# One scratch tile per FFN block and four smaller placements in a hybrid encoder layer

## The chip, the cores and the metric

The kernel runs on one NeuronCore of a Trainium2 chip. The metric is the device time of one execution in microseconds, as the median of the runs. The engines are named as in the profile: PE is TensorE's matmul stream and PEld its weight loads, DVE is VectorE, ACT is ScalarE, POOL is GpSimd, SP is SyncE, which here only issues transfers. Each engine works through its own instructions in order and waits on semaphores for the others. Transfers that SP issues run on the DMA queue q1, those that POOL issues on q0, and those that ACT issues on q10. All share the core's 16 DMA engines.

## The reference, cut to what matters

Two request groups (256 and 512 tokens, 768 rows in all, D = 1024) go through one encoder layer with the same weights:

```
h = RMSNorm(x);  u, q, k, v, qm, gl = split(h @ w_in)
z = gelu(bidirectional S5 scan of u + d*u)
s5_out   = z * sigmoid(z @ s5_w_glu)
diff_out = differential attention(q, k, v)          # 8 heads
mem_out  = cross-attention(qm, memory)              # 4 heads
merged   = sum over the branches n of sigmoid(gl[n] + b) * (out[n] @ w_branch[n])
x  = x + merged @ w_out                             # residual rows
h2 = RMSNorm(x);  g, up = split(h2 @ w_gate_up)     # 2 x 2816 columns
x  = x + (silu(g) * up) @ w_down                    # 2816 x 1024
```

## The kernel before

Everything is float32. A product is done as three matmuls on operands that are split into a high and a low part (`mm3`, lines 751 to 753: high by high, high by low, low by high). `split_evac` (lines 742 to 746) makes such a pair: ACT writes the high part, DVE the low part as the difference. In this way z becomes zhi and zlo, a left factor of the down projection dxh and dxl, its weights whd and wld. Activations are kept by features: a tile has 128 partitions and 8 blocks of 768 tokens.

The Tile framework places tiles in pools and puts the instructions of each engine in an order by its own simulation of the time. A pool that opens over SBUF bytes of an older pool inherits that pool's last users: the first tile of the new pool waits for all of them.

**The middle of the kernel.** Branch 2 (the memory branch, `br` over H) runs while differential attention is finished beside it. `finish(h)` transposes a head's output on PE (`oT`, line 1333), scales it on ACT into the tile `do` (line 1334), and ACT issues its store to the scratch `br_scr` (line 1335). Then comes the GLU of the S5 branch, `glu = z @ s5_w_glu`: `load_pair` loads the eight z tiles from scratch (names `brr`, POOL's queue, line 1525), half through the pool zst and half through the pool stg, and splits them. One `brr` buffer is free again when DVE has made its zlo. The `zs` tiles are z once more for the product with the sigmoid. After that come branch 0 (`br` over the GLU's result, with `glr` tiles of gates on POOL's queue), branch 1 (over xd, the differential attention's output loaded back from `br_scr`), the output projection `wo` and the FFN. The residual rows x1 (six tiles of 512 KB, line 1563) are needed at `wo`.

**The FFN and the down projection.** Eleven blocks of the hidden layer are made one after the other. POOL does the last products of a block in its tile `fa` (pool ffa, two buffers), and SP stores it to the scratch `hid_scr` (`hid_store`, line 1425). The down projection is a Strassen-like scheme: the 768 tokens are two halves r, the 22 feature groups of 128 two halves kh, the output columns two halves, and seven products P1, P5, P6, P3, P7, P2, P4 take the place of eight. Each product has six granules g of up to two feature groups. For a granule `a_load` loads a piece of the hidden layer (`da{r}{kh}_{g}`, from `hid_scr`, SP's queue), `w_fetch` loads a piece of w_down and may add a second piece to it with an accumulating load on POOL's queue (line 1733): the tiles `dch` for P5, P6 and P4, `dwr` for the others. `make` forms and splits the factors, AHEAD granules before PE needs them, and the matmuls `dn` take the left factor as the stationary operand and 512 weight columns as the moving one. FETCH says how many granules ahead weights are loaded. Granules 0 to 2 of P1 have their own small pool (dae) and are loaded while the last FFN block runs; all other da tiles lie in the pool downa, which opens when the FFN's pools close.

```
GRAN = [(k, min(2, NFB - k)) for k in range(0, NFB, 2)]
nc.sync.dma_start(t, hid_scr[:, NFB * kh + k0 : NFB * kh + k0 + n, HT * r : HT * r + HT])
load_pair(Z, z_scr, 0.5, (2, 3, 4, 7))
```

Of the kernel before, what the change touches and what calls it, by code (L numbers as in the profile page):

```python
# [8 lines left out]
F32 = mybir.dt.float32  # L9
# [477 lines left out]
TOK = 768  # L487
SEGS = ((0, 256), (256, 512))
TILES = 6
# [137 lines left out]
def hybrid_block(ctx, tc, A, outs, consts):  # L627
    nc = tc.nc
    v, act, gp, pe = nc.vector, nc.scalar, nc.gpsimd, nc.tensor
# [4 lines left out]
    xs = [A["x_prompt"][0, 128 * i : 128 * i + 128] for i in range(2)]  # L634
# [81 lines left out]
    NFB = DFF // 256  # L716
    wd = A["w_down"].rearrange("(k p) c -> p k c", p=128)
# [106 lines left out]
    k2 = qctx.enter_context(tc.tile_pool(name="ma2", bufs=2, side="right"))  # L824
# [3 lines left out]
    y_scr = [dr.tile([128, 8 * 97], F32, name=f"y_scr{m}") for m in range(8)]  # L828
    z_scr = [dr.tile([128, TOK], F32, name=f"z_scr{m}") for m in range(8)]
    gl_scr = [dr.tile([128, TOK], F32, name=f"gl_scr{m}") for m in range(24)]  # L830
    hid_scr = dr.tile([128, 2 * NFB, TOK], F32, name="hid_scr")
    br_scr = [dr.tile([128, TOK], F32, name=f"br_scr{m}") for m in range(8)]
    mo_scr = [dr.tile([128, 8, TOK], F32, name=f"mo_scr{w}") for w in "hl"]

# [136 lines left out]
    with tc.tile_pool(name="nrm", bufs=1) as pool, tc.tile_pool(name="nrmg", bufs=1) as pg:  # L971
# [274 lines left out]
    def diff_attend():  # L1246
# [79 lines left out]

        def finish(h):
            osb = X.pop(("h", h))[0]
            do = stg.tile([128, TOK], F32, name=uid("do"), tag="do", bufs=1)
            for t0, t1 in ((0, 2), (2, 6)):  # L1330
                ps = env.psb("oT")
                for t in range(t0, t1):
                    pe.transpose(ps[:, 128 * (t - t0) : 128 * (t - t0) + 128], osb[:, t], env.ident)
                act.activation(do[:, 128 * t0 : 128 * t1], ps[:, 0 : 128 * (t1 - t0)], AF.Copy, scale=subg)
            act.dma_start(br_scr[h], do)
# [75 lines left out]
    HT = TOK // 2  # L1411
# [10 lines left out]
        eng.tensor_tensor(out=o, in0=o, in1=c, op=mul)  # L1422

    def hid_store(fb):
        nc.sync.dma_start(hid_scr[:, 2 * fb : 2 * fb + 2, :], act_in.pop(fb))

    def new_block(what, fb):
        if what == "gate":
# [51 lines left out]
    with ExitStack() as c5:  # L1480
# [35 lines left out]
                                               in1=MG[0][:, M].bitcast(F32), op0=mul, op1=sub)  # L1516

        zctx = c5.enter_context(ExitStack())
        zst = zctx.enter_context(tc.tile_pool(name="zst", bufs=2, side="right"))

        def load_pair(X, src, scale=None, more=()):
            for m in range(8):
# [36 lines left out]
                split_evac(S[0][:, M], S[1][:, M], t, 0.25)  # L1559
        Xd = pair(XB, "xd")  # L1560
        load_pair(Xd, br_scr)
        for t in range(TILES):
            gp.dma_start(x1[t], xs[t])
        branch(0, S)
        MG = pair(XA, "mgd")
        branch(1, Xd, MG=MG)
        mgctx.close()
# [121 lines left out]


    P1, P5, P6, P3, P7, P2, P4 = range(7)
    GRAN = [(k, min(2, NFB - k)) for k in range(0, NFB, 2)]
    NG = len(GRAN)
    ITEMS = [(p, g) for p in range(7) for g in range(NG)]
    AHEAD, FETCH = 2, 4
    EARLY = 3
    de = ctx.enter_context(ExitStack())
    da_f = de.enter_context(tc.tile_pool(name="daf", bufs=3, side="right"))
    da_e = de.enter_context(tc.tile_pool(name="dae", bufs=1, side="right"))
    DP, a_raw, ch, w_raw, parts = {}, {}, {}, {}, {}  # L1700

    def a_load(q, g):

        k0, n = GRAN[g]
        r, kh = q
        early = q == (0, 0) and g < EARLY
        t = (da_e if early else DP["a"]).tile([128, 2, HT], F32, name=f"da{r}{kh}_{g}")[:, 0:n]
        nc.sync.dma_start(t, hid_scr[:, NFB * kh + k0 : NFB * kh + k0 + n, HT * r : HT * r + HT])
        a_raw[q, g] = t

    def w_quarter(kh, f, g):
        k0, n = GRAN[g]
        return wd[:, NFB * kh + k0 : NFB * kh + k0 + n, 512 * f : 512 * f + 512]

    def w_fetch(i):

        if i >= len(ITEMS):
            return
        p, g = ITEMS[i]
        n = GRAN[g][1]  # L1720
        view = lambda t: t.rearrange("p (k c) -> p k c", k=2)[:, 0:n]
        if p in (P5, P6, P4):
            if p == P5:
                ch[g] = view(DP["ch"].tile([128, 1024], F32, name=f"dch{g}"))
                nc.sync.dma_start(ch[g], w_quarter(0, 0, g))
            t = ch[g]
            src, acc = None, {P5: (0, 1), P6: (1, 1), P4: (1, 0)}[p]
        else:
            t = view(W.praw.tile([128, W.HALF], F32, name=f"dwr{i}", tag="wr"))
            src, acc = {P1: ((0, 0), None), P3: ((1, 1), None), P7: ((0, 1), (1, 1)), P2: ((1, 0), None)}[p]  # L1730
            nc.sync.dma_start(t, w_quarter(*src, g))
        if acc:
            gp.dma_start(t, w_quarter(*acc, g), accum_op=add)
        w_raw[i] = t

    def make(i):
# [1 line left out]
        if i >= len(ITEMS):  # L1738
            return
        p, g = ITEMS[i]  # L1740
        n = GRAN[g][1]
        t = w_raw.pop(i)
        wh, wl = (x.rearrange("p (k c) -> p k c", k=2)[:, 0:n] for x in W.tiles(f"d{i}"))
        split_evac(wh, wl, t)
# [23 lines left out]
        parts[i] = xh, xl, wh, wl  # L1768

    def down_early():  # L1770
        for i in range(FETCH - 1):
            w_fetch(i)
        for g in range(EARLY):
            a_load((0, 0), g)
        for i in range(AHEAD):
            make(i)
# [6 lines left out]
    xbctx.close()  # L1783

    with ExitStack() as c7:
        for k, n in (("a", 1), ("ch", 1), ("t", 2)):
            DP[k] = c7.enter_context(tc.tile_pool(name="down" + k, bufs=n))
        loads = [((0, 0), g) for g in range(EARLY, NG)]
        loads += [(q, g) for g in range(NG) for q in ((1, 0), (1, 1))] + [((0, 1), g) for g in range(NG)]
# [2 lines left out]
        acc = {}  # L1792
        for _ in range(NG - EARLY):
            a_load(*loads.pop(0))
        w_fetch(FETCH - 1)
        for i, (p, g) in enumerate(ITEMS):
            for _ in range(3):
                if loads:
# [4 lines left out]
            if g == 0 and p in (P1, P5, P2):  # L1803
                acc[bank] = [PS[bank].tile([128, 512], F32, name=uid("dn"), tag=bank) for _ in range(3)]
            ps = acc[bank]
            n = GRAN[g][1]
            xh, xl, wh, wl = parts.pop(i)
            for t in range(3):
                c = slice(128 * t, 128 * t + 128)
# [55 lines left out]
```

## Time and profile before

| | |
|---|---|
| time, median of 3 runs | 1800.16 us (1799.32 to 1803.69) |
| the profiled execution | 1803.27 us, of which the span of the trace is 1801.5 us |
| PE busy | 1751.7 us, 97% of the span |
| DVE, ACT, POOL busy | 1263.3, 886.6, 281.4 us |
| moved by DMA | 236.98 MB, 132 GB/s on average |
| q1 (SP), q0 (POOL) | 166.93 MB and 65.02 MB |

In the timeline a row has its start in us from the start of the span, its length, the engine and source line, and the operation as output <- input; in brackets the idle time before it and what ended that. A matmul's length runs to its modelled end, so the pace is read from one start to the next. The chain of waits follows back what released each instruction. A window's row gives for each engine the busy time and the count of instructions, then the granted clock of PE as a share of full speed, the share of the DMA engines and the GB/s.

### The profile page before, as it was taken

Reading aid. Unit: us, or ns where it says so; the run is one execution under the profiler, and the core shown is the slowest. Engines: PE = TensorE matmul, PEld = TensorE weight load, DVE = VectorE, ACT = ScalarE, POOL = GpSimd, SP = SyncE. Lnnn points to the kernel's source line nnn. Section 1 sums busy time; section 2 is a strip of 40 time slices with the busy share of each in tenths; the row PEclk is TensorE's granted clock in tenths of the full one; section 3 lists DMA queues with packets and bytes.
Section 4 is the critical chain, followed back from the end, with each engine's and each line's share of the span. In section 5 each row is a group of like instructions: output and inputs, shape, how many; then the busy total and the mean of one; then the engine's idle time right before and its main releaser. Section 6 shows DMA issues by size and latency. Waiting matters only on the chain.

```text
span 1801.5 us, 29429 instructions
## 1 busy us (share of the span) xinstructions
PE 1751.7 (97%) x11194; PEld 1611.7 (89%) x11194; DVE 1263.3 (70%) x2342; ACT 886.6 (49%) x1856; POOL 281.4 (16%) x300
## 2 busy tenths in 40 slices
PE   9999999999999999999989899999999999996999
PEld 9999988999999999999979788888889999994877
DVE  6665659699999688888865435452797777764854
ACT  6444444677676267777755333232343333332442
POOL 0000000000000001011100101000136555541210
PEclk9999999999999999999999899999999999997999
DMA  7223745664565565454843535322223232349781
GB/s 264 71 83 106 141 110 138 150 160 119 146 154 139 139 168 146 93 112 107 192 127 100 193 105 181 115 94 70 71 85 123 88 117 90 107 164 300 144 204 47
DMA packets 211166, 236.98 MB, mean 132 GB/s; under 512 B 57929, under 2 KB 173393, under 8 KB 211025
## 3 DMA queue, kind: packets, MB, share of 16 engines
q1 hardware_dynamic: 185584, 166.93, 30.5%
q0 software_dynamic: 24288, 65.02, 16.9%
q10 hardware_dynamic: 1152, 3.15, 0.5%
q8 instruction: 88, 1.44, 0.3%
q14 instruction: 54, 0.43, 0.1%
HBM read 168.66 MB, written 41.22 MB: 117 GB/s over the span
## 4 chain that ended last, share of the span: by engine, by line
PE 52%; DMA 5%; DVE 4%; issue 2%; ACT 1%; POOL 0%; SPq 0%; DVEq 0%; ACTq 0%; POOLq 0%
PE br L752 4%; PE br L751 4%; PE br L753 3%; PE up L751 3%; PE up L752 3%; PE up L753 3%; PE gate L751 3%; PE gate L753 3%; PE gate L752 3%; PE dn L751 2%; PE dn L753 2%; PE dn L752 2%; PE av L1311 2%; PE qk L752 2%; PE qk L751 2%
## 5 line engine op out<-in xcount | busy, mean ns | idle before, releaser
L595 ACT ACTIVATE wh<-wr 128x1024 fp32r<-128x1024 f32 x124 | 140.4, 1133 | 63.3 <-PE br L752 18.1
L601 DVE TENSOR_TENSOR wl<-wr,wh 128x1024 fp32r<-128x1024 f32 x82 | 108.3, 1324 | 81.3 <-ACT wh L595 79.4
L751 PE MATMUL gl<-Hhi,wh 128*128 128x256 f32 (+1 forms) x384 | 133.0, 346 | 2.3 <-ACT glt L1114 2.3
L753 PE MATMUL gl<-Hhi,wl 128*128 128x256 f32 (+1 forms) x384 | 129.7, 338 | 0.0
L752 PE MATMUL gl<-Hlo,wh 128*128 128x256 f32 (+1 forms) x384 | 129.4, 337 | 0.0
L751 PE MATMUL qk<-wh,Hhi 128*128 128x256 f32 x384 | 108.7, 283 | 0.7 <-ACT V L1210 0.7
L752 PE MATMUL qk<-wl,Hhi 128*128 128x256 f32 x384 | 109.3, 285 | 0.0
L751 PE MATMUL dn<-whd,dxh 128*128 128x512 f32 x231 | 92.5, 402 | 17.3 <-ACT dxh L745 17.3
L753 PE MATMUL qk<-wh,Hlo 128*128 128x256 f32 x384 | 108.5, 283 | 0.0
L599 POOL DMA_DIRECT2D wl<-wr x42 | 36.6, 872 | 454.8 <-ACT wl L598 427.7
L752 PE MATMUL dn<-wld,dxh 128*128 128x512 f32 x231 | 92.4, 401 | 0.1
L753 PE MATMUL dn<-whd,dxl 128*128 128x512 f32 x231 | 89.8, 400 | 0.7 <-DVE dxl L746 0.7
L751 PEld LDWEIGHTS gl<-Hhi,wh 128*128 128x128 f32 x384 | 72.8, 190 | 9.7 <-ACT glt L1114 2.7
L753 PEld LDWEIGHTS gl<-Hhi,wl 128*128 128x128 f32 x384 | 72.7, 189 | 8.0
L752 PEld LDWEIGHTS gl<-Hlo,wh 128*128 128x128 f32 x384 | 72.9, 190 | 7.2
L1280 DVE TENSOR_REDUCE nm<-sc 128x1 f32<-128x512 f32 (+1 forms) x96 | 56.5, 598 | 26.2 <-PE sc L1275 25.1
L751 PEld LDWEIGHTS qk<-wh,Hhi 128*128 128x128 f32 x384 | 73.2, 191 | 1.6 <-ACT V L1210 0.9
L753 PEld LDWEIGHTS qk<-wh,Hlo 128*128 128x128 f32 x384 | 73.4, 191 | 0.3
L752 PEld LDWEIGHTS qk<-wl,Hhi 128*128 128x128 f32 x384 | 72.9, 190 | 0.6
L557 ACT ACTIVATE wh_S<-ws 128x512 fp32r<-128x512 f32 x70 | 41.1, 625 | 59.5 <-PE up L752 33.3
L751 PEld LDWEIGHTS dn<-whd,dxh 128*128 128x128 f32 x231 | 44.1, 191 | 29.0 <-ACT dxh L745 18.5
L558 DVE TENSOR_TENSOR wl_S<-ws,wh_S 128x512 fp32r<-128x512 f32 x70 | 57.8, 849 | 15.2 <-ACT wh_S L557 15.2
(476 smaller groups left out, 6025.3 us busy)
## 6 DMA issues: line engine op xcount, KB each, us to landing
wr<-in_w_in_dram SPq DMA_DIRECT2D x48, 512.0 KB, 4.7
wr<-in_w_gate_up_dram SPq DMA_DIRECT2D x44, 512.0 KB, 3.6
wl<-wr POOLq DMA_DIRECT2D x42, 512.0 KB, 5.2
wr<-in_w_branch_dram SPq DMA_DIRECT2D x24, 512.0 KB, 4.4
dwr<-in_w_down_dram SPq DMA_DIRECT2D x20, 512.0 KB, 4.0
glr<-gl_scr POOLq DMA_DIRECT2D x24, 384.0 KB, 3.6
hid_scr<-fa SPq DMA_DIRECT2D x11, 768.0 KB, 6.5
wr<-in_w_mem_kv_dram SPq DMA_DIRECT2D x16, 512.0 KB, 3.5
```

The costliest lines, as they stand in the source:

```text
L557: self.nc.scalar.activation(f(hi), src, AF.Copy)
L558: self.nc.vector.tensor_tensor(out=f(lo), in0=src, in1=f(hi).bitcast(F32), op=ALU.subtract)
L595: self.nc.scalar.activation(hi, r, AF.Copy)
L599: self.nc.gpsimd.dma_start(lo, r.bitcast(F32R), accum_op=ALU.add)
L601: self.sub.tensor_tensor(out=lo, in0=r, in1=hi.bitcast(F32), op=ALU.subtract)
L751: pe.matmul(ps, wh, xh, start=start, stop=False, **kw)
L752: pe.matmul(ps, wh, xl, start=False, stop=False, **kw)
L753: pe.matmul(ps, wl, xh, start=False, stop=stop, **kw)
L1280: v.tensor_reduce(out=nm[:, m : m + 1], in_=ps, axis=AX.X, op=ALU.max, negate=True)
L1311: pe.matmul(po[:, 0:128], aT[:, 128 * k : 128 * k + 128], V[:, c0 // 128 + k, 128 * (h % 2) : 128 * (h % 2) + 128], start=(k == 0), stop=( ...
```

## The change

Five edits:

- `hid_scr` is no longer one DRAM tile with 22 feature groups, but eleven tiles, one per block. The two feature halves of the down projection now run along blocks: kh = 0 is blocks 0 to 4 and the first half of block 10, kh = 1 is blocks 5 to 9 and the second half of block 10. `granule` gives the block, the first group and the count.
- FETCH goes from 4 to 6, and P7's weights get a pool of their own (`downr`, three tiles `dwt`); the fetches before the pools open stay three.
- The residual rows x1 are loaded in branch 0, before its second weight, and not ahead of branch 0.
- zst has three buffers, and the tile `do` goes from the pool stg to the pool k2 (da2 in the orders).
- A 64-byte tile `dgap` is placed first on the right side, so that the left factors (pool daf) and the early da tiles lie 64 bytes lower: the left factors at 210848 in place of 210912.

```diff
-    hid_scr = dr.tile([128, 2 * NFB, TOK], F32, name="hid_scr")
+    hid_scr = [dr.tile([128, 2, TOK], F32, name=f"hid_scr{fb}") for fb in range(NFB)]
...
-            do = stg.tile([128, TOK], F32, name=uid("do"), tag="do", bufs=1)
+            do = k2.tile([128, TOK], F32, name=uid("do"), tag="do", bufs=1)
...
-        nc.sync.dma_start(hid_scr[:, 2 * fb : 2 * fb + 2, :], act_in.pop(fb))
+        nc.sync.dma_start(hid_scr[fb], act_in.pop(fb))
...
-        zst = zctx.enter_context(tc.tile_pool(name="zst", bufs=2, side="right"))
+        zst = zctx.enter_context(tc.tile_pool(name="zst", bufs=3, side="right"))
...
         load_pair(Xd, br_scr)
-        for t in range(TILES):
-            gp.dma_start(x1[t], xs[t])
-        branch(0, S)
+
+        def rows_in(c):
+            if c == 1:
+                for t in range(TILES):
+                    tc.keep_in_program_order(gp.dma_start(x1[t], xs[t]))
+
+        branch(0, S, hook=rows_in)
...
-    GRAN = [(k, min(2, NFB - k)) for k in range(0, NFB, 2)]
-    NG = len(GRAN)
+    NG = NFB // 2 + 1
+
+    def granule(kh, g):
+        if g < NG - 1:
+            return (NG - 1) * kh + g, 0, 2
+        return NFB - 1, kh, 1
+
...
-    AHEAD, FETCH = 2, 4
+    AHEAD, FETCH = 2, 6
...
+    de.enter_context(tc.tile_pool(name="dgap", bufs=1, side="right")).tile([128, 16], F32, name="dgap")
...
-        nc.sync.dma_start(t, hid_scr[:, NFB * kh + k0 : NFB * kh + k0 + n, HT * r : HT * r + HT])
+        nc.sync.dma_start(t, hid_scr[fb][:, m : m + n, HT * r : HT * r + HT])
...
-            t = view(W.praw.tile([128, W.HALF], F32, name=f"dwr{i}", tag="wr"))
+            t = view(DP["r"].tile([128, 1024], F32, name=f"dwt{i}", tag="dwt") if p == P7 else
+                     W.praw.tile([128, W.HALF], F32, name=f"dwr{i}", tag="wr"))
...
-        for i in range(FETCH - 1):
+        for i in range(3):
             w_fetch(i)
...
-        for k, n in (("a", 1), ("ch", 1), ("t", 2)):
+        for k, n in (("a", 1), ("ch", 1), ("t", 2), ("r", 3)):
...
-        w_fetch(FETCH - 1)
+        for i in range(3, FETCH):
+            w_fetch(i)
```

The framework's order moves with this at three places. SP's queue where the FFN ends and the down projection begins, before and then after (dch, dwr and dwt are pieces of w_down, hid_scr the store of the last block, da the pieces of the hidden layer; the number behind dwr and dwt is the item, six a product in the order P1, P5, P6, P3, P7, P2, P4):

```order
L1725 DMA dch4_17926<-in_w_down_dram 128x2x512
L1725 DMA dch5_17959<-in_w_down_dram 128x512
L1731 DMA dwr5_17762<-in_w_down_dram 128x512
L1731 DMA dwr18_18151<-in_w_down_dram 128x2x512
L1425 DMA hid_scr_164<-fa_1786_17421 128x1536
L1731 DMA dwr19_18180<-in_w_down_dram 128x2x512
L1731 DMA dwr20_18209<-in_w_down_dram 128x2x512
L1708 DMA da00_3_17711<-hid_scr_164 128x2x384
```

```order
L1735 DMA dch4_17889<-in_w_down_dram 128x2x512
L1735 DMA dch5_17925<-in_w_down_dram 128x512
L1742 DMA dwt24_18284<-in_w_down_dram 128x2x512
L1742 DMA dwr5_17738<-in_w_down_dram 128x512
L1742 DMA dwt25_18315<-in_w_down_dram 128x2x512
L1742 DMA dwt26_18346<-in_w_down_dram 128x2x512
L1742 DMA dwr18_18114<-in_w_down_dram 128x2x512
L1425 DMA hid_scr10_174<-fa_1786_17435 128x1536
L1742 DMA dwr19_18143<-in_w_down_dram 128x2x512
L1742 DMA dwr20_18172<-in_w_down_dram 128x2x512
L1718 DMA da00_3_17728<-hid_scr3_167 128x2x384
```

Three weight loads of P7 now stand ahead of the last block's store; the store, dwr19, dwr20 and da00_3 follow one another as they did. In both orders da00_3 waits for the semaphore of that store.

POOL's queue where the GLU begins, before and then after (glr are gates, x1 the residual rows, brr z tiles 4 to 7, zs z once more):

```order
L1499 DMA glr_1413_12343<-gl_scr23_163 128x768
L1563 DMA x1_0_12232<-in_x_prompt_dram 128x1024
L1563 DMA x1_1_12233<-in_x_prompt_dram 128x1024
L1563 DMA x1_2_12234<-in_x_sample_dram 128x1024
L1563 DMA x1_3_12235<-in_x_sample_dram 128x1024
L1563 DMA x1_4_12236<-in_x_sample_dram 128x1024
L1563 DMA x1_5_12237<-in_x_sample_dram 128x1024
L1525 DMA brr_1407_12263<-z_scr5_137 128x768
L1525 DMA brr_1408_12267<-z_scr6_138 128x768
L1525 DMA brr_1406_12259<-z_scr4_136 128x768
L1525 DMA brr_1409_12271<-z_scr7_139 128x768
L1553 DMA zs_1419_12413<-z_scr0_132 128x768
```

```order
L1499 DMA glr_1413_12353<-gl_scr23_163 128x768
L1525 DMA brr_1407_12273<-z_scr5_137 128x768
L1525 DMA brr_1408_12277<-z_scr6_138 128x768
L1525 DMA brr_1409_12281<-z_scr7_139 128x768
L1553 DMA zs_1419_12423<-z_scr0_132 128x768
```

The six x1 loads have left this place (they now stand between a glr and a brr of br_scr in branch 0), and z4 has gone ahead of the last gates.

ACT at the same place, before and then after (do is the last head's output, br_scr7 its store, wh45 the second GLU weight, zhi the splits of z0, z1 and so on):

```order
L1334 ACTIVATE do_1390_12051<-oT_1391_12052,subg_90 128x256
L1334 ACTIVATE do_1390_12051<-oT_1392_12056,subg_90 128x512
L745 ACTIVATE zhi_1400_12241<-brr_1402_12243 128x768
L745 ACTIVATE zhi_1400_12241<-brr_1403_12247 128x768
L745 ACTIVATE zhi_1400_12241<-brr_1404_12251 128x768
L745 ACTIVATE zhi_1400_12241<-brr_1405_12255 128x768
L1335 DMA br_scr7_172<-do_1390_12051 128x768
L595 ACTIVATE wh45_0_12400<-wr45_0_12115 128x1024
L595 ACTIVATE wh45_1_12406<-wr45_1_12280 128x1024
```

```order
L595 ACTIVATE wh45_0_12410<-wr45_0_12125 128x1024
L1334 ACTIVATE do_1390_12061<-oT_1391_12062,subg_90 128x256
L1334 ACTIVATE do_1390_12061<-oT_1392_12066,subg_90 128x512
L1335 DMA br_scr7_182<-do_1390_12061 128x768
L595 ACTIVATE wh45_1_12416<-wr45_1_12290 128x1024
L745 ACTIVATE zhi_1400_12251<-brr_1402_12253 128x768
L745 ACTIVATE zhi_1400_12251<-brr_1403_12257 128x768
L745 ACTIVATE zhi_1400_12251<-brr_1404_12261 128x768
L745 ACTIVATE zhi_1400_12251<-brr_1405_12265 128x768
L745 ACTIVATE zhi_1400_12251<-brr_1406_12269 128x768
```

One weight tile has moved ahead of do, the other ahead of the splits, and the first zhi now waits for the store of do. On PE the transposes oT that do reads stand six matmuls later among the last `br` group than they did.

More of the change, by code (lines that the diff above doesn't have):

```diff
@@ L1702, in a_load @@
     def a_load(q, g):
-        k0, n = GRAN[g]
         r, kh = q
+        fb, m, n = granule(kh, g)
         early = q == (0, 0) and g < EARLY
         t = (da_e if early else DP["a"]).tile([128, 2, HT], F32, name=f"da{r}{kh}_{g}")[:, 0:n]
-        nc.sync.dma_start(t, hid_scr[:, NFB * kh + k0 : NFB * kh + k0 + n, HT * r : HT * r + HT])
+        nc.sync.dma_start(t, hid_scr[fb][:, m : m + n, HT * r : HT * r + HT])
         a_raw[q, g] = t
     def w_quarter(kh, f, g):
-        k0, n = GRAN[g]
-        return wd[:, NFB * kh + k0 : NFB * kh + k0 + n, 512 * f : 512 * f + 512]
+        fb, m, n = granule(kh, g)
+        return wd[:, 2 * fb + m : 2 * fb + m + n, 512 * f : 512 * f + 512]
     def w_fetch(i):
@@ L1719, in w_fetch @@
         p, g = ITEMS[i]
-        n = GRAN[g][1]
+        n = granule(0, g)[2]
         view = lambda t: t.rearrange("p (k c) -> p k c", k=2)[:, 0:n]
@@ L1740, in make @@
         p, g = ITEMS[i]
-        n = GRAN[g][1]
+        n = granule(0, g)[2]
         t = w_raw.pop(i)
@@ L1805, in hybrid_block @@
             ps = acc[bank]
-            n = GRAN[g][1]
+            n = granule(0, g)[2]
             xh, xl, wh, wl = parts.pop(i)
```

## The prediction

> **What bounds the kernel now.** I read the page's busy times and slices first, then the waits of TensorE, then the chain around each of its long waits, then the DMA queues inside those stretches.
>
> ```profile
> PE 1751.7 (97%) x11194; PEld 1611.7 (89%) x11194; DVE 1263.3 (70%) x2342; ACT 886.6 (49%) x1856; POOL 281.4 (16%) x300
> PEclk9999999999999999999999899999999999997999
> ```
>
> TensorE works 97% of the span, so a change pays only where it waits, where its clock is halved, or where one matmul gets shorter. The clock row dips twice. Both dips lie behind a long wait (timeline of PE: start, duration, idle before and releaser):
>
> ```profile
> 1007.54 0.28 PE L753 MATMUL glu<-zhi,wl 128*128 128x256 f32 x1
> 1016.48 1.22 PE L751 MATMUL glu<-zhi,wh 128*128 128x256 f32 x3 [8.66 <-ACT zhi L745]
> ...
> 1020.20 0.63 PE L751 MATMUL glu<-zhi,wh 128*128 128x512 f32 x1
> 1020.63 0.45 PE L752 MATMUL glu<-zlo,wh 128*128 128x512 f32 x1
> ...
> 1625.63 0.40 PE L753 MATMUL dn<-whd,dxl 128*128 128x512 f32 x1
> 1642.61 0.79 PE L751 MATMUL dn<-whd,dxh 128*128 128x512 f32 x1 [16.58 <-ACT dxh L745]
> ```
>
> A shorter wait before them, and windows around all three (windows: the last three columns are granted clock, DMA share, GB/s):
>
> ```profile
> 909.95 0.47 PE L752 MATMUL br<-Hlo,wh 128*128 128x512 f32 x1 [2.83 <-DMA Hlo<-mo_scrl]
> ...
> 903.00:911.00 8.00, 5.02 (x36) 4.66 (x37) 1.56 (x4) 1.81 (x8) 0.00 (x0) 1.00 0.87 237
> 1010.00:1021.00 11.00, 4.52 (x16) 3.90 (x17) 3.83 (x4) 3.38 (x4) 1.07 (x2) 0.53 0.83 301
> 1030.00:1240.00 210.00, 209.96 (x1173) 183.11 (x1172) 91.85 (x121) 64.98 (x84) 15.59 (x29) 1.00 0.36 118
> 1642.00:1649.00 7.00, 6.39 (x15) 5.00 (x16) 2.48 (x3) 1.92 (x3) 0.00 (x0) 0.52 1.09 296
> ```
>
> The change works at both places. The second wait, where the FFN ends and the down projection needs its fourth left factor, hangs on a chain of transfers (chain of waits: start, duration, what):
>
> ```profile
> 1618.55 1.05 POOL fa L1422
> 1619.62 10.23 DMA hid_scr<-fa
> 1629.90 11.71 DMA da<-hid_scr
> 1641.71 0.85 ACT dxh L745
> ```
>
> The last store of the hidden activations takes 10.23 us, and only then is the first load from that scratch issued, which takes 11.71 us.
>
> **The change part by part.**
>
> *Scratch per block, halves along blocks.* This should let da00_3 (block 3) be loaded without waiting for block 10's store. It doesn't: the pool of the da tiles lies over SBUF that the ffa pool held, block 10's tile among it, and in the changed order da00_3 still waits for the semaphore of the hid_scr10 store. Worth 0.
>
> *Three more weight tiles fetched early (FETCH 6, pool downr).* Their loads (dwt24 to dwt26, 512 KB each, 1.57 MB) now stand on SP's queue ahead of that store, and their three accumulating loads on POOL's queue behind those of dch. What shares the wires there (DMA views of 1612 to 1619 and of 1626 to 1644: packets, MB, share):
>
> ```profile
> q1 hardware_dynamic: 1342, 2.58, 100.8%
> ...
> q0 software_dynamic: 1256, 2.41, 72.1%
> q1 hardware_dynamic: 1250, 2.21, 37.6%
> ```
>
> Alone, SP's queue q1 moves 2.58 MB in 7 us, 0.37 MB/us. Beside POOL's accumulates on q0 it moves 1250 packets in 18 us, 69 a microsecond, as many as q0. Three loads with rows of 512 floats (2,048 bytes) are 768 packets: 768/69 = 11.1 us. In the trace q1 held 100.8% of the engines in the 7 us before the store's issue, so at 1619.6 the added bytes still stand ahead of the store. Sharing doesn't end sooner either: q0 gets the same 768 packets. Store and da00_3 each keep their own duration and land 11.1 us later, and the 16.58 us wait becomes about 27.7. Bounds: 4.3 us if the loads ran at the unshared rate (1.57/0.37); 15 us if the second round of da loads is pressed as well, taken as another third. I take +11.1, since the transfers of this very stretch give it. P7, whose weights these are, makes TensorE wait nowhere now, so the earlier fetch earns nothing.
>
> *Residual rows moved.* POOL issued them ahead of four z loads (timelines of POOL and ACT):
>
> ```profile
> 998.50 1.06 POOL L1563 DMA_DIRECT2D x<-in_x_prompt_dram  x2 [14.10 <-ACT do L1334]
> 999.55 2.09 POOL L1563 DMA_DIRECT2D x<-in_x_sample_dram  x4
> 1004.07 0.54 POOL L1525 DMA_DIRECT2D brr<-z_scr  x1 [1.37 <-DMA x<-in_x_prompt_dram]
> ...
> 1001.38 2.00 ACT L595 ACTIVATE wh<-wr 128x1024 fp32r<-128x1024 f32 x2
> 1013.18 0.84 ACT L745 ACTIVATE zhi<-brr 128x768 fp32r<-128x768 f32 x1 [9.80 <-DMA brr<-z_scr]
> 1015.59 0.84 ACT L745 ACTIVATE zhi<-brr 128x768 fp32r<-128x768 f32 x1 [0.37 <-DMA brr<-z_scr]
> ```
>
> Six loads of 512 KB stand in front of z: that is the 8.66 us wait. Behind it TensorE runs at half clock, from 1016.48 to 1020.63 (1020.20 to 1020.63: 0.43 us from one 512-column matmul to the next, where 0.23 is usual), which loses half of 4.15, 2.1 us. At the new place the same 3.15 us of POOL issue stand ahead of glr and br_scr loads. What hides them is branch 0, where TensorE is busy 209.96 of 210 us, with gate tiles loaded ahead in two buffers. I take 0; without that cover it would be the 3 us of issue.
>
> *Three z staging tiles, and `do` in the da2 pool.* z0 to z4 are now there early. But z's own tiles lie over da2, so the first zhi now waits until the last `do` has been stored. That store comes later than before: in the new order TensorE transposes oT six matmuls later, and ScalarE converts a weight tile ahead of `do`. Rows for the times (PE, ACT, DVE, the DMA issues of 996 to 1018, and the br_scr tiles over the whole run):
>
> ```profile
> 995.84 0.40 PE L751 MATMUL br<-Hhi,wh 128*128 128x512 f32 x1
> 997.00 0.82 PE L1333 MATMUL oT<-ident,osb 128*128 128x128 f32 x6
> 997.58 0.48 PE L753 MATMUL br<-Hhi,wl 128*128 128x512 f32 x1
> 1002.03 0.51 PE L751 MATMUL glu<-zhi,wh 128*128 128x256 f32 x2
> ...
> 997.42 1.13 ACT L1334 ACTIVATE do<-oT,subg 128x256 f32<-128x256 f32 x2 [8.09 <-PE oT L1333]
> ...
> 999.31 3.56 DVE L746 SCALAR_TENSOR_TENSOR zlo<-brr,zhi 128x768 fp32r<-128x768 f32 x4 [2.85 <-ACT zhi L745]
> ...
> br_scr<-do ACTq DMA_DIRECT2D x1, 384.0 KB, 2.9
> ...
> DMA to landing us min/median/max: 2.3/3.5/5.3
> ```
>
> oT at 997.00 + 6 x 0.23 = 998.4. ScalarE's weight tile 998.6 to 999.6, `do` 1.13 to 1000.7, store 2.9 to 1003.6, zhi 0.84 to 1004.4. TensorE, free at 1002.03, waits 2.4 us, then some 0.4 more for zlo (0.89 a tile). z5 to z7 are issued as zlo frees tiles, from 1005.3 on, and a 384 KB load with nothing beside it takes about that 2.9 us, while TensorE needs 1.4 us for each z tile (four in the 5.6 us from 1002.03), so k = 5 is wanted at 1012: in time. The wait of 8.66 becomes 2.8 in two pieces, and I expect full clock behind it, since the wait of 2.83 us that ended at 909.95 left the clock of 903 to 911 at 1.00. Gain 8.66 - 2.8 + 2.1 = 8.0. Bounds: 10.8 if zhi needn't wait at all; 3.5 if the store takes the 5.3 us of the slowest br_scr transfer and the half clock stays.
>
> The page "TensorE: Matmul & The Clock Gate" of the Trainium skill (HAM oscillation) asks for no idle above about 3.4 us. By it my wait is safe by 0.6 us, and a store slower by that much would give the 2.1 us back; no run here shows the threshold between 2.8 and 8.7 us.
>
> *Left factors 64 bytes lower.* These tiles go from 96 to 32 bytes past a multiple of 128. Two streams of 512-column matmuls at full clock, first and last row of each, the first with left factors at the old offset, the second with both operands at 32, and the page's row for the count:
>
> ```profile
> 1621.67 0.39 PE L751 MATMUL dn<-whd,dxh 128*128 128x512 f32 x1
> 1625.40 0.39 PE L752 MATMUL dn<-wld,dxh 128*128 128x512 f32 x1
> ...
> 1185.83 0.39 PE L752 MATMUL br<-xdlo,wh 128*128 128x512 f32 x1
> 1187.42 0.39 PE L753 MATMUL br<-xdhi,wl 128*128 128x512 f32 x1
> ...
> L751 PE MATMUL dn<-whd,dxh 128*128 128x512 f32 x231 | 92.5, 402 | 17.3 <-ACT dxh L745 17.3
> ```
>
> 3.73/16 = 0.233 us against 1.59/7 = 0.227. With 693 dn matmuls (three groups of 231) the new offset is worth 693 x 0.006 = 4.2 us if it is the address that makes the difference, 0 if it is anything else in that stage. I take 4.2, as other streams pair with their offsets in the same way.
>
> The same page (Back-to-back issue gap) gives a matmul N/2.4 + 2.5 ns, 215.7 ns for 512 columns, with no term for addresses; by it the edit is worth 0. The trace has 233 and 227, both above, so something the rule lacks is at work.
>
> **Sum.** +11.1 - 8.0 - 4.2 + 0 + 0 = -1.1 us. The profiled execution took 1803.27 us (span 1801.5), 3.1 above the median of 1800.16; on the median the forecast is 1799.0. What a measurement of this kernel can tell from no change is about 0.3%, 5.4 us, so this is no change: a shorter wait at z paid for with a longer one at the down projection.
>
> **The rivals.**
>
> 1. *The down wait doesn't grow* (the three loads fit in without moving the store, or the split does free da00_3). For: the scratch tiles are separate now. Against: order and semaphore. Without growth -12.2, 1788; with the 10.23 us of the store out of the chain, 1778.
> 2. *Loads become the bound in the down projection.* Place: P5's da loads, already late by 11 us, run against the second round of dch accumulates, which POOL issued from 1655.30 on (row below). Price 11.1 + 4 to 8 in place of 11.1. It decides once da10 and da11 land later than TensorE has finished P1. For: DMA share 1.09 here. Against: q1 is back at full rate once q0 pauses, and all of it shifts together. 1803 to 1807, and slower if the address edit brings nothing besides.
>
> ```profile
> 1655.30 1.20 POOL L1733 DMA_DIRECT2D dch<-in_w_down_dram  x1 [25.43 <-DVE wld L743]
> ```
>
> 3. *The z wait stays long* because zhi hangs on the store of `do`: idle over the clock's threshold, gain 3.5 in place of 8.0, with the address worth 0 also: 1799.0 + 4.5 + 4.2 = 1808, slower.
> 4. *The address does nothing* (what the skill's formula says): 1803.2, within 0.3%.
>
> **How the numbers follow.** Forecast 0.36 (its own range 1794 to 1804), rival 1 0.21, rival 2 0.17, rival 3 0.16, rival 4 0.10. Faster: rival 1 and a tenth from the forecast's low end, 0.31. Slower: rival 3, rival 2 nearly whole and a little of the others, 0.34. Same: 0.35. Leaving out the outer part of rival 1 and the worst of 2 and 3 gives 1786 to 1810.
>
> **What would show it.** Right: TensorE's wait for zhi 2 to 3 us with no clock dip behind it; its wait for dxh 26 to 29 us, with the chain store, da load as before and dwt loads ahead of it; dn matmuls 0.227 apart. Wrong: a dxh wait at or under 17 us (then the queue sharing or the kept wait is misread), a clock dip near 1005, dn matmuls still 0.233 apart, or waits for da inside P5.

## The result, and the profile after

| | before | changed |
|---|---|---|
| median of 13 runs each | 1800.95 us (1796.74 to 1807.73) | 1798.33 us (1795.85 to 1801.27) |
| ratio | | 0.9983, 95% interval 0.9972 to 0.9994 |
| profiled execution, and its span | 1803.27 us, 1801.5 us | 1797.81 us, 1796.0 us |
| first long wait (z) | 8.66 us | 2.14 us |
| second long wait (down projection) | 16.58 us | 29.55 us |

The change is worth -0.17%, or -3.1 us (1800.95 x 0.0017), within the 0.3% that was called no change. The two long waits moved by -6.5 and +13.0 us. The page of the changed kernel gives TensorE's busy time (first row), its clock (second) and the group of the first `dn` product (third):

```profile
PE 1742.0 (97%) x11194; PEld 1608.4 (90%) x11194; DVE 1262.5 (70%) x2342; ACT 887.0 (49%) x1856; POOL 280.7 (16%) x300
PEclk9999999999999999999999999999999999996999
L751 PE MATMUL dn<-whd,dxh 128*128 128x512 f32 x231 | 90.8, 394 | 29.6 <-ACT dxh L745 29.6
```

One of the two dips of the clock row is gone, the other is a tenth deeper. A slice of that row is 45 us wide, so a shorter dip needs a narrower view. PE's timeline at z and at the down projection:

```profile
999.28 0.40 PE L753 MATMUL br<-Hhi,wl 128*128 128x512 f32 x1
1001.82 0.88 PE L751 MATMUL glu<-zhi,wh 128*128 128x256 f32 x3 [2.14 <-ACT zhi L745]
...
1004.04 0.63 PE L753 MATMUL glu<-zhi,wl 128*128 128x512 f32 x1
1004.47 0.63 PE L751 MATMUL glu<-zhi,wh 128*128 128x512 f32 x1
...
1643.82 0.79 PE L751 MATMUL dn<-whd,dxh 128*128 128x512 f32 x1 [29.55 <-ACT dxh L745]
...
1648.98 0.39 PE L751 MATMUL dn<-whd,dxh 128*128 128x512 f32 x1
...
1655.78 0.39 PE L751 MATMUL dn<-whd,dxh 128*128 128x512 f32 x1
...
1657.54 0.50 PE L753 MATMUL dn<-whd,dxl 128*128 128x512 f32 x1 [1.15 <-DVE dxl L746]
```

Four readings. The z wait is 2.14 us. Behind it two 512-column matmuls start 0.43 us apart (1004.04, 1004.47): half clock all the same, until 1005.66. The down wait is 29.55 us. From 1648.98 to 1655.78 lie 30 matmuls, 0.227 us each. The last row is a small wait inside P5 that the kernel before did not have.

Windows of the changed kernel (the last three columns are granted clock, DMA share, GB/s), behind the z wait, in branch 0 and late in the down projection; and, in a fence of its own, the last one of the kernel before:

```profile
1001.82:1005.82 4.00, 3.89 (x14) 3.13 (x15) 4.00 (x5) 2.88 (x4) 1.61 (x3) 0.57 0.69 208
1030.00:1240.00 210.00, 210.00 (x1155) 182.56 (x1154) 94.33 (x124) 67.33 (x86) 18.20 (x34) 1.00 0.39 131
1700.00:1750.00 50.00, 50.00 (x223) 41.40 (x222) 36.08 (x44) 23.55 (x28) 3.31 (x3) 1.00 0.53 148
```

```profile
1700.00:1750.00 50.00, 48.50 (x204) 37.70 (x203) 30.85 (x37) 20.59 (x25) 6.92 (x6) 1.00 0.72 179
```

The moved residual rows hold nothing up in branch 0 (210.00 of 210 us). In the last window TensorE now has no idle time, where it had 1.50 us before.

Where the 5.5 us between the two profiled spans lie can be told in four pieces, cut at the start of branch 2's 512-column matmuls and at both ends of the down wait:

| piece | before | changed | difference |
|---|---|---|---|
| start to `br` | 903.15 | 901.07 | -2.1 |
| `br` to the down wait | 722.88 | 713.20 | -9.7 |
| down wait | 16.58 | 29.55 | +13.0 |
| restart to the end | 158.89 | 152.18 | -6.7 |

TensorE's instructions are the same in the first piece, so its 2.1 us are one execution against another. Over the profiled executions below, that same point lies between 900.43 and 904.30. A difference of a few us between two spans proves nothing alone; a wait or a pitch read in both traces does. In the second piece z brings 6.9 us, shorter wait and shorter half clock together. Another 1.6 us are two waits early in the FFN, here in PE's waits in the kernel before:

```profile
PE up L751 <- DVE fs L1458: 0.8, 1, 0.8
PE gate L752 <- DVE flo L743: 0.8, 1, 0.8
```

The changed kernel has neither. What the remaining 1.2 us are was not traced.

### The profile page after: what moved, and what is told of

Same layout as the page of the kernel before. It is cut to its first block, busy times and chain, and to the rows that moved or that the text cites. A ratio compares the mean times of both kernels' runs of the same rounds, so it can differ in the third digit from the quotient of the medians.

```text
span 1796.0 us, 29428 instructions
## 1 busy us (share of the span) xinstructions
PE 1742.0 (97%) x11194; PEld 1608.4 (90%) x11194; DVE 1262.5 (70%) x2342; ACT 887.0 (49%) x1856; POOL 280.7 (16%) x300
## 4 chain that ended last, share of the span: by engine, by line
PE 57%; DMA 4%; DVE 2%; issue 1%; SPq 1%; ACT 0%; POOL 0%; DVEq 0%; ACTq 0%; POOLq 0%
PE br L752 4%; PE br L751 4%; PE br L753 4%; PE gate L751 3%; PE gate L752 3%; PE up L752 3%; PE gate L753 3%; PE up L751 3%; PE up L753 3%; PE dn L753 3%; PE dn L751 3%; PE dn L752 3%; PE av L1311 2%; PE qk L752 2%; PE qk L751 2%; PE qk L753 2%
## 5 line engine op out<-in xcount | busy, mean ns | idle before, releaser
L745 ACT ACTIVATE dxh<-da 128x768 fp32r<-128x768 f32 (+1 forms) x36 | 28.5, 792 | 93.9 <-PE dn L752 49.4
```

Source lines behind the costliest of these rows:

```text
L745: act.activation(hi, src, AF.Copy, scale=scale)
```

## The experiments

Each kernel is the one before or the changed one with one part done, undone or altered. A ratio is against runs of the kernel before on the same chip, with its 95% interval.

**z: all of its edits, and the row loads alone.** `z_only` is the kernel before with three of the edits:

```diff
-            do = stg.tile([128, TOK], F32, name=uid("do"), tag="do", bufs=1)
+            do = k2.tile([128, TOK], F32, name=uid("do"), tag="do", bufs=1)
-        zst = zctx.enter_context(tc.tile_pool(name="zst", bufs=2, side="right"))
+        zst = zctx.enter_context(tc.tile_pool(name="zst", bufs=3, side="right"))
-        for t in range(TILES):
-            gp.dma_start(x1[t], xs[t])
-        branch(0, S)
+        branch(0, S, hook=rows_in)
```

> The kernel before with the z edits alone: residual rows moved into branch 0, three z staging tiles, do in the da2 pool. My theory (the six row loads ahead of z made the 8.66 us wait, and the half clock behind it goes with it): the wait of glu for zhi is 2 to 3 us, no half clock after it, the down projection as before with a 16 to 17 us wait for dxh, time 8 to 9 us below the kernel before. Rival (the z loads are slow for another reason, or the store of do holds zhi for long): a wait of 5 us or more, half clock kept, gain under 4 us.

Measured: 0.9942 (0.9920 to 0.9963). The z wait was 2.15 us, with half clock behind it again.

`x1_only` has the last of these edits alone: two staging tiles, `do` where it was.

> The kernel before with one edit of the z part alone: the six row loads moved into branch 0; z staging (two tiles) and do stay as before. If the row loads alone made the wait: z4 to z7 land before TensorE wants them, the wait of glu for zhi is under 1 us (no wait for the store of do here), no half clock, 10 to 13 us below the kernel before, at least as much as the three z edits together. Rival (two staging tiles are too few): a wait of 3 us or more stays.

Measured: 0.9949 (0.9936 to 0.9962). Waits of PE around z in x1_only (in all, times, longest):

```profile
PE glu L751 <- ACT zhi L745: 0.5, 1, 0.5
```

and the window behind that wait:

```profile
999.00:1022.00 23.00, 22.23 (x128) 19.24 (x127) 14.39 (x15) 12.31 (x17) 3.77 (x7) 1.00 0.59 201
```

The wait is shorter than with all three edits, and the clock stays at 1.00. So moving the row loads carries the whole gain at z. The gain in time, 9.2 us (6.9 to 11.5), is a little under the 10 to 13 that were expected. The third staging tile and the new place of `do` add nothing that the times show (the intervals overlap). In the traces they cost the longer wait and the half clock at z, and they take away the two waits early in the FFN: of the fourteen profiled executions only the three kernels with these two edits (`z_only`, `no_fetch` and the changed one) are without them. ACT's timeline of the changed kernel shows what zhi waits for.

```profile
996.07 1.06 ACT L595 ACTIVATE wh<-wr 128x1024 fp32r<-128x1024 f32 x1 [9.00 <-PE br L752]
997.03 1.03 ACT L1334 ACTIVATE do<-oT,subg 128x256 f32<-128x256 f32 x2
998.10 0.33 ACTq L1335 DMA_DIRECT2D br_scr<-do  x1
999.48 1.06 ACT L595 ACTIVATE wh<-wr 128x1024 fp32r<-128x1024 f32 x1 [1.42 <-PE br L752]
1000.92 2.31 ACT L745 ACTIVATE zhi<-brr 128x768 fp32r<-128x768 f32 x3 [0.38 <-DMA br_scr<-do]
```

From the issue of the store of `do` at 998.10 to zhi at 1000.92 are 2.8 us; the z tiles themselves have been there. The store ends the wait, but only by 0.38 us: the second weight tile, which itself waits 1.42 us for TensorE, keeps ACT until 1000.54. By this timeline zhi would come only some 0.4 us sooner without the store.

**The address alone.** `gap_only` is the kernel before with one line:

```diff
+    de.enter_context(tc.tile_pool(name="dgap", bufs=1, side="right")).tile([128, 16], F32, name="dgap")
```

> The kernel before with the 64-byte gap alone. Address theory: dn matmuls start 0.227 us apart in place of 0.233, 3.5 to 4.5 us faster, nothing else changed. Rival (a matmul's pace has no term for addresses and the pace in the down projection comes from its transfers): 0.233 us, no change.

Measured: 0.9980 (0.9968 to 0.9992), -3.6 us (-5.8 to -1.4). Two rows of its PE timeline, seven starts apart:

```profile
1648.93 0.39 PE L751 MATMUL dn<-whd,dxh 128*128 128x512 f32 x1
...
1650.52 0.39 PE L752 MATMUL dn<-wld,dxh 128*128 128x512 f32 x1
```

1.59/7 = 0.227 us, in a kernel in which nothing but the addresses of the left factors and of the early da tiles was changed. In the traces of all kernels with that line the median distance from one `dn` matmul to the next at full clock is 0.227 us, in all others 0.233.

**The earlier fetch alone, and everything but it.** `fetch_only` is the kernel before with FETCH 6 and the pool downr; `no_fetch` is the changed kernel without these:

```diff
-    AHEAD, FETCH = 2, 6
+    AHEAD, FETCH = 2, 4
-            t = view(DP["r"].tile([128, 1024], F32, name=f"dwt{i}", tag="dwt") if p == P7 else
-                     W.praw.tile([128, W.HALF], F32, name=f"dwr{i}", tag="wr"))
+            t = view(W.praw.tile([128, W.HALF], F32, name=f"dwr{i}", tag="wr"))
-        for k, n in (("a", 1), ("ch", 1), ("t", 2), ("r", 3)):
+        for k, n in (("a", 1), ("ch", 1), ("t", 2)):
```

> The kernel before with FETCH 6 and the separate P7 pool alone, one scratch tile kept. Queue theory: the three weight loads ahead of the last store put 11 to 13 us on the wait for dxh (27 to 30 us), time 11 to 13 us above the kernel before. Rival (the longer wait of the changed kernel comes from the new halves of the hidden layer or the separate scratch tiles): the wait stays at 16 to 18 us and the time within 2 us of before.

> The changed kernel with the fetch edit undone (FETCH 4, P7 weights in the shared pool); the other four edits stay. Queue theory: wait for dxh 16 to 18 us again, 12 to 14 us below the kernel before, some 1787. Rival (scratch split or new halves cost too): the wait stays above 20 us. If the separate scratch tiles did free da00_3, the wait would fall under 10 us.

Measured: `fetch_only` 1.0050 (1.0034 to 1.0066), its down wait 28.6 us; `no_fetch` 0.9923 (0.9904 to 0.9943), its down wait 17.3 us. The chains of waits, fetch_only first, then no_fetch:

```profile
1620.63 22.87 DMA hid_scr<-fa
1643.58 11.67 DMA da<-hid_scr
```

```profile
1610.82 10.94 DMA hid_scr<-fa
1622.39 11.13 DMA da<-hid_scr
```

Against 10.23 and 11.71 us before, the store is 12.6 us longer with the fetch and 0.7 without it, and the da load keeps its length: the queue ahead of the store, as forecast. The changed kernel's own DMA issues of 1606 to 1614 say the same (the last number is the time to landing):

```profile
hid_scr<-fa SPq DMA_DIRECT2D x1, 768.0 KB, 23.2
```

Its DMA queues from 1614 to 1632, while that store is under way (packets, MB, share):

```profile
q0 software_dynamic: 1150, 2.20, 66.0%
q1 hardware_dynamic: 1150, 2.72, 43.4%
```

1150 packets on each queue in 18 us, 64 a microsecond: packet for packet. The Trainium skill says as much ("DMA: Bandwidth & Descriptors", Queues, rings and completion order): each DMA engine takes its queues in turn, a packet at a time. The equal counts agree with it, 1150 to 1150; whether the profile counts the same thing as a packet as the page does is not shown.

But `fetch_only` costs 9.0 us (6.1 to 11.9), less than its 12 us of longer wait. From the restart to the end it takes 154.9 us in place of 158.89, so it gives 4.0 back. Some 1.1 of these are half clock: it lasts 4.0 us behind the restart, in place of 6.2. The rest lies in P7. PE's timeline of the kernel before:

```profile
1737.68 0.40 PE L753 MATMUL dn<-whd,dxl 128*128 128x512 f32 x1
1738.78 0.50 PE L751 MATMUL dn<-whd,dxh 128*128 128x512 f32 x1 [0.70 <-ACT dxh L745]
1739.31 0.50 PE L752 MATMUL dn<-wld,dxh 128*128 128x512 f32 x1
1740.17 0.50 PE L753 MATMUL dn<-whd,dxl 128*128 128x512 f32 x1 [0.37 <-DVE dxl L746]
...
1745.79 0.39 PE L751 MATMUL dn<-whd,dxh 128*128 128x512 f32 x1
```

and its waits of 1735 to 1748:

```profile
ACT whd L742 <- DMA dwr<-in_w_down_dram: 10.3, 3, 5.2
```

From the first row of the timeline to its last are 22 starts in 8.11 us, where 22 x 0.233 would be 5.13: 3.0 us lost at the beginnings of two granules, behind a weight tile that ACT waited for. The brackets show only a part of it, since a row's length runs to a modelled end: 1738.78 to 1739.31 is 0.53 us from start to start and has no bracket. In fetch_only and in the changed kernel PE has no wait there.

**Without P7's accumulates.** `fetch_noacc` is fetch_only with this edit, by which P7's weights lack their second piece:

```diff
-        if acc:
+        if acc and p != P7:
```

> The kernel before with the fetch edit, but P7's six accumulating loads on POOL's queue are left out (P7's weights then lack a summand); the early loads on SP's queue stay. If it is the queue ahead of the store that costs (my theory): the wait for dxh stays at 25 to 29 us, a little under 28.6 since POOL's queue ends sooner. If it is POOL's accumulates that hold the wires: the wait falls to 17 to 20 us.

Measured: 1.0036 (1.0023 to 1.0050), down wait 24.8 us, just under the range of the first theory and far above that of the second. Its chain of waits:

```profile
1621.82 20.94 DMA hid_scr<-fa
1642.84 7.85 DMA da<-hid_scr
```

With POOL's three accumulates away the store is 1.9 us shorter and the da load 3.8. The larger part of the store's +12.6, some 10.7 us, stays: that part is the loads ahead of it on SP's queue.

**The stall without the wait for the store.** `split_onescr` is the kernel before, with its one scratch tile, and the da tiles in two pools, so that the first of them does not lie over the FFN's tiles:

```diff
-        t = (da_e if early else DP["a"]).tile([128, 2, HT], F32, name=f"da{r}{kh}_{g}")[:, 0:n]
+        t = (da_e if early else DP["a" if len(a_raw) < EARLY + 16 else "b"]).tile([128, 2, HT], F32, name=f"da{r}{kh}_{g}")[:, 0:n]
-        for k, n in (("a", 1), ("ch", 1), ("t", 2)):
+        for k, n in (("a", 1), ("b", 1), ("ch", 1), ("t", 2)):
```

> The kernel before, with its one scratch tile, with only this edit: the pool of the da tiles is cut in two, so that the first 16 tiles lie below the bytes of the ffa pool. Theory (the overlap in SBUF keeps da00_3 behind the last store, the scratch tile does not): da00_3 is loaded ahead of the store, the wait for dxh falls from 16.6 to under 4 us, no half clock behind it, 13 to 19 us below the kernel before. Rival 1 (one scratch tile holds the loads back): the wait stays near 16. Rival 2 (the loads of P5 become the bound): the wait goes but 5 us or more come back as waits inside P5.

Measured: 1.0020 (1.0010 to 1.0030). da00_3, the first of the da loads that used to wait, is now issued ahead of the last store although the scratch is still one tile (SP's timeline):

```profile
1615.70 8.63 SPq L1708 DMA_DIRECT2D da<-hid_scr  x6
1624.43 3.28 SPq L1425 DMA_DIRECT2D hid_scr<-fa  x1
```

So it was the shared SBUF bytes that held it, not the scratch, and eleven scratch tiles free nothing. The long wait goes, but others come up in P1 and P5, as the second rival had it. The waits for dxh in its PE timeline:

```profile
1629.54 0.50 PE L751 MATMUL dn<-whd,dxh 128*128 128x512 f32 x1 [1.27 <-ACT dxh L745]
1643.87 0.59 PE L751 MATMUL dn<-whd,dxh 128*128 128x512 f32 x1 [3.53 <-ACT dxh L745]
1652.43 0.50 PE L751 MATMUL dn<-whd,dxh 128*128 128x512 f32 x1 [2.36 <-ACT dxh L745]
...
1675.74 0.80 PE L751 MATMUL dn<-whd,dxh 128*128 128x512 f32 x1 [8.58 <-ACT dxh L745]
```

and the da loads in its chain of waits:

```profile
1636.50 19.39 DMA da<-hid_scr
1655.91 17.86 DMA da<-hid_scr
```

Together 15.7 us in 4 waits, against 16.6 in one, and da loads of 18 to 19 us in place of 11.7. Behind the wait for the store stands a second bound of nearly the same size. The DMA engines are full all along (a share of 1.06 to 1.10 from 1615 to 1676), so it is the loads; whether it is their bytes or their order on the queues is not shown.

`best_x` joins this split with the moved row loads and the address:

> The kernel before with the row loads in branch 0, the 64-byte gap and the da pool cut in two; no scratch split, no fetch edit, no z staging edit. If the three terms add: 10.5 + 3.6 + 16 = 30, some 27 to 33 us below the kernel before. If the da loads then collide with the accumulates: 20 to 26.

Measured: 0.9953 (0.9937 to 0.9970), 15.8 us of down waits in 6. No gain from the split.

**The useful parts alone.** `xg` is the kernel before with two edits, the row loads in branch 0 and the 64 bytes:

> The kernel before with the row loads in branch 0 and the 64-byte gap, nothing else. If the terms add: 9 to 11 plus 3.6, some 13 to 15 us below the kernel before, the same as the changed kernel without its fetch edit; wait for dxh 16 to 17 us. If the scratch split or the z staging had a part in that result: 3 us or more short of it.

Measured: 0.9935 (0.9921 to 0.9948), 1790.08 against 1801.47 us, down wait 16.0 us. It is as fast as `no_fetch`, which also has eleven scratch tiles, the new halves, the third staging tile and the moved `do`.

**Another order of products.** P2 needs no accumulating loads and comes second, in `p2_split` with the two da pools, in `p2_nosplit` without; the da loads follow that order:

```diff
-    P1, P5, P6, P3, P7, P2, P4 = range(7)
+    P1, P2, P5, P6, P3, P7, P4 = range(7)
```

> As xg, with the da pool cut in two, and the product P2 computed second in place of sixth: it needs one left factor and no accumulating load, so fewer bytes are wanted between the FFN and the third product. If the bytes wanted there are the bound: the waits of dn, 16 us in sum with the pool cut alone, fall under 8, and the time is 20 us or more below the kernel before. If what holds is the order of the queues (the dch loads and accumulates still go first, P2's weights come behind them): waits of 12 us or more stay and the time is that of xg or above.

> As xg, with P2 second, da pool uncut. da00_3 still waits for the last store: the wait for dxh stays at 16 to 18 us, time within 4 us of xg; waits behind it if P2's weights come late.

Measured: 0.9931 (0.9919 to 0.9944) and 0.9923 (0.9905 to 0.9941). Waits of PE in p2_split:

```profile
PE dn L751 <- ACT whd L742: 14.3, 2, 12.7
PE dn L751 <- ACT dxh L745: 1.6, 1, 1.6
```

The factors are there, and now P2's weights are late, by as much. That is the second of the two outcomes expected, the order of the queues, but it does not clear the bytes: with the DMA engines full here too, the two were not told apart. In p2_nosplit the wait for dxh is 16.4 us as ever. Neither can be told from `xg`.

**P7's weights early, but not ahead of the store.** `p7_late` is xg with FETCH 6 and the pool downr, its loads kept behind the da loads on SP's queue:

```diff
+            d = nc.sync.dma_start(t, w_quarter(*src, g))
+            if p == P7:
+                tc.keep_in_program_order(d)
```

> Both useful edits (row loads in branch 0, left factors 64 bytes lower) and P7's weights in their own pool with FETCH 6, but their loads kept behind the da loads on SP's queue, where they follow P3's last weight. Theory (the early fetch costs only through its place ahead of the last store, and it earns what P7 loses at its granule starts): the dxh wait stays at 16 to 17.5 us with the store at 8 to 11 us, TensorE's waits in P7 go, and against the kernel with the two edits alone (0.9935 of before, dxh wait 16.0) some 2.7 us come off: 0.991 to 0.993 of before. Rival (P7's waits left the changed kernel because its weights were loaded in the long stall, when nothing else was wanted): placed here the loads share the wires with what P6 and P3 want, the P7 waits stay at 2 to 3 us or turn up in P3, and the time stays at 0.9935 or above.

Measured: 0.9932 (0.9917 to 0.9947). The down wait is 15.9 us and the store 7.79, each just under what was expected. The waits in P7 are still there (PE's timeline):

```profile
1728.15 0.50 PE L751 MATMUL dn<-whd,dxh 128*128 128x512 f32 x1 [2.20 <-ACT dxh L745]
1729.55 0.50 PE L753 MATMUL dn<-whd,dxl 128*128 128x512 f32 x1 [0.36 <-DVE dxl L746]
```

The waits of 1690 to 1790 name a weight tile of P7 (dwt), and the window of 1700 to 1750 has 2.6 us without a matmul:

```profile
ACT whd L742 <- DMA dwt<-in_w_down_dram: 15.3, 4, 9.1
```

```profile
1700.00:1750.00 50.00, 47.41 (x200) 38.27 (x199) 28.99 (x34) 20.02 (x26) 6.37 (x6) 0.97 0.71 180
```

By these waits the rival held; the time lies between the two forecasts and decides nothing. So the 3 us in P7 were had because its weights were loaded in the long stall, at a cost of 9 to 12 us, and this order of loads does not bring them. Which of the loads in front makes P7's weights late in this kernel was not tried.

## Why the prediction was right, and where it was not

The forecast was no change, 1799.0 us, as a shorter wait at z against a longer one at the down projection. 1798.33 us was measured, and a shorter wait against a longer one is what the traces show. That the sum came so near is in part luck: two steps failed, the clock behind z and the worth of the fetch, each by some 2 us and in opposite directions. Term by term:

- **Scratch per block, new halves: 0, and it was 0.** `no_fetch` and `xg` differ by these and by the staging edits, and are equal within their intervals. The reason given, the SBUF bytes that the da pool shares with the FFN's tiles, is shown by `split_onescr`, where one scratch tile holds nothing back.
- **Loads ahead of the last store: +11.1 forecast, +12 to +13 measured** (28.6 and 29.55 against 16.58 us). The mechanism was right. The term was 768/69; the queues moved 64 packets a microsecond beside each other here, and 768/64 = 12.0. That POOL's accumulates cost nothing extra on the da load ("sharing doesn't end sooner either") is not quite so: without them the da load takes 7.85 in place of 11.67 us. But in the kernel before other accumulates shared with it, at 11.71.
- **"the earlier fetch earns nothing": the step that failed.** It rested on "P7 makes TensorE wait nowhere now". The row that I quoted for the count of `dn` held the contradiction: 17.3 us of idle time in all, of which the long wait is 16.58. The other 0.7 us was in P7, and the pitch there shows 3.0 us. The fetch as a whole costs 9.0 us (6.1 to 11.9), not 11.1; by the trace of `fetch_only` it is 12.1 - 4.0 = 8.1.
- **z: of the 2.8 us forecast, 2.4 were for zhi, and that wait is 2.14.** The reason given (zhi waits for the store of `do`) is in the trace, and from the store's issue to zhi it was 2.8 us where 2.9 was taken. But the prediction had left out the second weight tile, which now stands on ACT between the store and zhi and ends only 0.38 us before zhi starts.
- **"full clock behind it": failed.** It rested on the one wait of 2.83 us without a drop, and length is not what decides (below). TensorE ran at half clock from 1002.24 to 1005.66, the dip near 1005 that was named as a sign of being wrong; it loses 1.7 of the 2.1 us counted as gain. By the traces z brought 8.66 - 2.14 + 0.4 = 6.9 us, not 8.0, and the two waits early in the FFN, which were not forecast, 1.6 more. By the times, `z_only` brought 10.4 us (6.7 to 14.4), which holds all of these. The row loads alone would have kept the clock: they cost nothing in branch 0, as forecast, and the gain at z is theirs.
- **The address: -4.2 forecast, -3.6 measured** (1.4 to 5.8). The rival by which it does nothing fell, and with it, as a forecast for this stream, the formula of the Trainium skill ("TensorE: Matmul & The Clock Gate", Back-to-back issue gap), which the page gives for a single matmul in isolation: the pitch went from 0.233 to 0.227 us by the address alone.
- **Not in the forecast:** the half clock behind the down wait was shorter (3.6 us in place of 6.1, 1.3 us less lost), and the 1.15 us wait in P5, behind a late da load; waits for da there were another sign of being wrong. These two nearly cancel.

With the measured parts, -10.4 - 3.6 + 9.0 = -5.0 us against -3.1 (-5.0 to -1.1) for the whole: the parts add up within their intervals. The pieces read in the traces, with the address at 693 x 0.006 = 4.2, give -6.9 - 1.6 - 4.2 + 13.0 - 3.0 - 1.3 + 1.15 = -2.85. Without the fetch, -10.4 - 3.6 = -14.0 against -13.9 for `no_fetch`.

Of the rivals, the first (the down wait doesn't grow) fell. The second (loads are the bound) is not what the changed kernel shows, apart from 1.15 us, but it is right about the stage: `split_onescr` and `p2_split` take the wait for the store away, and waits for loads of 16 us in sum remain.

## What to carry to other kernels

A load that is issued early is paid for by whatever stands behind it on its queue: ask which store or load that is, and whether an engine waits for it. Before you call a stage free of waits, read its pitch from start to start against the same matmuls elsewhere, and see that the group's idle time is used up by the waits you know. When a wait hangs on one transfer in a stretch where the DMA engines are full, ask what else is still to be loaded there: taking that dependence away bought nothing here.

## What the runs showed of the hardware

**The clock drops behind shorter waits than thought, and where a wait falls decides.** Before the result, the trace had one wait of 2.83 us with no drop. At the same place, behind the wait for Hlo, two waits of one length ended differently: the changed kernel kept its clock and xg lost it. Changed kernel, a row of PE's timeline and the window of the next 4 us (granted clock third from the end):

```profile
907.50 0.47 PE L752 MATMUL br<-Hlo,wh 128*128 128x512 f32 x1 [2.45 <-DMA Hlo<-mo_scrl]
```

```profile
907.50:911.50 4.00, 4.00 (x18) 3.29 (x19) 0.00 (x0) 0.00 (x0) 0.00 (x0) 1.00 0.02 6
```

The same row of xg, and the window of its half clock:

```profile
910.73 0.54 PE L752 MATMUL br<-Hlo,wh 128*128 128x512 f32 x1 [2.45 <-DMA Hlo<-mo_scrl]
```

```profile
911.00:914.41 3.41, 3.41 (x9) 2.65 (x8) 0.00 (x0) 0.00 (x0) 0.00 (x0) 0.50 0.01 4
```

The half clock behind z in the changed kernel:

```profile
1002.24:1005.66 3.42, 3.31 (x12) 2.56 (x11) 3.42 (x5) 2.46 (x4) 1.61 (x3) 0.50 0.77 225
```

Over the fourteen profiled executions the drop came at Hlo behind 2.45, 2.55 (three times), 2.61, 2.77, 2.82, 2.90 and 2.97 us, and not behind 2.31, 2.45, 2.46, 2.64 and 2.83; at z it came behind 2.14 and twice behind 2.15. So no length of the wait decides it between 2.1 and 2.9 us.

The clock records in the traces show what does. Within an execution all changes of the granted clock lie whole multiples of 3.41 us apart; both stretches above are one such piece of time. In xg the wait, 908.28 to 910.73, lies inside the piece that ends at 911.00 and fills 72% of it. In the changed kernel the wait, 905.05 to 907.50, is cut at 906.67 and fills 47% of one piece and 24% of the next, while the 2.14 us at z fill 63% of one. Counted over the fourteen traces, with each matmul taken at its usual pitch, all 54 pieces behind which the clock fell were empty by 57% or more, and behind every piece at full clock that was empty by 61% or more it fell. Short gaps add up: in P7 of xg it fell behind a piece whose longest wait in brackets is 0.89 us.

The Trainium skill's rule of idle gaps under 3.4 us ("TensorE: Matmul & The Clock Gate", HAM oscillation) does not keep a kernel safe by these runs, where 2.14 us were enough. Another part of the page (Part 1: The HAM clock gate) says that activity is watched in a window of about 3.4 us that runs freely; the pieces of 3.41 us, which lie differently against the program in each execution, agree with that.

**64 bytes of SBUF address change a matmul by 6 ns**, 0.233 to 0.227 us for 512 columns, when the left factor goes from 96 to 32 bytes past a multiple of 128. Why is open; other offsets were not tried.
